# A hybrid decoder layer on one core: two orders changed, token sums taken from ScalarE's copies, and pair 2 of the first feed-forward part computed as a block step

## The chip, the core and the metric

The kernel runs on one NeuronCore of a Trainium2 chip, in float32. The metric is the device time of one execution in microseconds. The core's engines work side by side, each through its own instructions in order: TensorE (PE) multiplies and transposes, VectorE (DVE) and ScalarE (ACT) do elementwise work, GpSimd (POOL) small things, and SyncE's queue (SP) issues nearly all transfers. They wait for each other through semaphores.

## The reference

A decoder layer for 512 tokens of width 1024: a SwiGLU feed-forward part, a token mixer, and a second feed-forward part, each between RMS norms.

```python
def rms_norm(x, g):
    xf = x.astype(jnp.float32)
    y = xf * lax.rsqrt(jnp.mean(xf * xf, axis=-1, keepdims=True) + RMS_EPS)
    return (y * g.astype(jnp.float32)).astype(x.dtype)

def swiglu(x, w_gate, w_up, w_down):
    return (jax.nn.silu(x @ w_gate) * (x @ w_up)) @ w_down
...
    def compress(t, pe, w1, w2):
        tb = t[:, blk_idx] + pe[None, None, :, None, :]
```

The feed-forward width is 2816, 22 tiles of 128. The mixer projects the normed tokens once and runs two kinds of attention on the result; of it only `compress` matters here: before its matmuls it adds a small position table `pe` to the keys and values.

## The kernel before, in words

**Three products for one.** Each float32 product is made of three matmuls of rounded parts (`mm3`, L128): high by high (L130), then the tokens' low part by the weights' high part (L131), then the tokens' high part by the weights' low part (L132). So every weight block is split first (`split`, L106): ACT casts the high part (L107), DVE subtracts it to get the low part (L108). Weight blocks come by DMA into three `raw` buffers of 1 MB; their parts go to three `whi`/`wlo` pairs.

**Tokens.** The tokens are normed and transposed in four tiles of 128 (`norm_steps`, L188): squares on ACT (L139), reciprocal root on DVE and POOL (`rstd`, L142, with L148 and L152), scaling on DVE (`scale`, L198, into `tmp`), eight transposes on PE (L203), cast on ACT (L206) into `xh`, rest on DVE (L210) into `xl`.

**The feed-forward parts** (`ffn`, L277) go through 22 f-tiles in 11 pairs. A classical pair (`classical`, L391) multiplies gate and up of two f-tiles over all 512 tokens, 24 matmuls 512 wide for each product. A block pair (`strassen`, L326) treats the pair as two by two blocks, and makes 7 products in place of 8, each of 24 matmuls 256 wide. For that it needs sums of the weights' quarters (L345, L347, L351 and others, on DVE) and four sums T1 to T4 of the tokens' quarters, made once for each part by `token_sums` (L472): join high and low part of a quarter (L494), subtract (L497), split (L108). `STRASSEN` says which pairs are block pairs: in part one from pair 3, in part two from pair 2. `STEPS` says how many steps of the token sums are put behind which f-tile. For later use the quarters of the down weights are summed as well (`down_sums`, L446, L449): for some pairs in the buffer of the raw weights, for others in free slots (`early_sums`, L451).

**The opening** (from L1400 on) interleaves by hand the loads, the norms of tiles 0 to 3 and the splits of the first weights. PE starts on the first half of the tokens (tiles 0 and 1) with gate and up of f-tile 0, then does tile 2's transposes, gate of f-tile 1, tile 3's transposes, up of f-tile 1, and the second half of the tokens after that. The transposes stand in `self.pending`.

**The mixer's start** has the same form (`nsa`, L1006): four projections over the first 256 tokens, with the transposes of tiles 2 and 3 among them, while part one's end is still being normed on DVE (L633, L640). Ahead of them stands `positions` (L748): it loads the position table, transposes it on PE (L754) and copies it on DVE (L756); `block_rows` and `blocks` (L758, L768) copy the projections and add the table (L776).

**What sets the order.** The program is written in one order, and a scheduler places each instruction on its engine by it and by the buffers: a tile under one tag takes the next free buffer of that tag, and waits for its last reader. Steps inside `issue_after` are put behind a given instruction.

Of the kernel before, what the change touches and what calls it, by code (L numbers as in the profile page):

```python
# [12 lines left out]
F32 = mybir.dt.float32  # L13
# [14 lines left out]
NF = DFF // P  # L28
# [17 lines left out]
T_TAGS = ["NN"] * 3 + ["N"] + ["PT"] * 8 + ["CB"]  # L46
STRASSEN = range(3, NF // 2), range(2, NF // 2)
AHEAD = {0: 10, 1: 9}
SUM_TAGS = {2: ["KB"] * 4, 3: ["x"] * 4, 4: ["x"] * 4, 5: ["V"] * 4, 6: ["x"] * 4, 7: ["V"] * 4,
            8: ["of"] * 2 + ["V"] * 2}  # L50
STEPS = (0, 3, 3, 3, 3), (4, 4, 4)
EARLY = 5
HOLD_TAGS = ["W"] * 2 + ["Q"] * 4 + ["KA"] * 2 + ["V"] * 2 + ["CB", "ring"]
PS_BUFS = dict(S=3, T=2, V=1, F=2)
PS_TAGS = [t for t in PS_BUFS for _ in range(PS_BUFS[t])]

OPEN = ("SS", "TT", "SS", "FF")
AFTER_FFN, AFTER_MIX = ("SS", "FF", "SS", "TT"), ("SS", "TT", "FF", "SV")


class Layer:
    def __init__(self, ctx, tc, a):
        self.tc, self.nc, self.a = tc, tc.nc, a
        self.pool = ctx.enter_context(tc.tile_pool(name="sb", bufs=1))
        self.psum = ctx.enter_context(tc.tile_pool(name="ps", bufs=1, space=PSUM))
        self.nps = 0
        self.consts()

# [118 lines left out]

    def norm_steps(self, t, pre, tags):  # L188

        nc = self.nc  # L190
        xn = self.sbt("tmp", [P, D], bufs=2)
        c = slice(t * P, (t + 1) * P)
        xh, xl = self.xht, self.xlt
        pt = {}

        def scale(h, r):
            hc = slice(h * S, (h + 1) * S)
            nc.vector.scalar_tensor_tensor(xn[:, hc], self.x[2 * t + h], r, pre[h], op0=OP.mult, op1=OP.mult)  # L198

        def transpose(h):  # L200
            pt[h] = self.bank(tags[h])
            for j in range(4):
                nc.tensor.transpose(pt[h][:, j * P:(j + 1) * P], xn[:, (4 * h + j) * P:(4 * h + j + 1) * P], self.ident)  # L203

        def cast(h):
            self.last_cast = nc.scalar.copy(xh[:, 4 * h:4 * h + 4, c], pt[h].rearrange("p (j c) -> p j c", j=4)).ins  # L206

        def rest(h):
            ks = slice(4 * h, 4 * h + 4)
            self.last_rest = nc.vector.tensor_sub(xl[:, ks, c], pt[h].rearrange("p (j c) -> p j c", j=4), xh[:, ks, c].bitcast(F32)).ins  # L210
        return scale, transpose, cast, rest

    def norm_T(self, t, pre, tags, sq=None):

        r = self.rstd(sq or self.squares(t))
        scale, transpose, cast, rest = self.norm_steps(t, pre, tags)
# [60 lines left out]
    def ffn(self, n, wg, wu, wd, post, finish, xsrc, tags, nps, aside=None):  # L277
# [113 lines left out]
        def classical(f, act):  # L391
# [11 lines left out]
            nc.vector.tensor_mul(act, act, bs[1])  # L403
            if f == 1:
                sums.extend(self.token_sums())
            if 1 <= f <= len(STEPS[n]):
                with self.tc.issue_after(self.last_rest):
                    for _ in range(STEPS[n][f - 1]):
                        sums.pop(0)()
# [62 lines left out]
    def token_sums(self):  # L472


        nc = self.nc
        H = S // 2
        places = []
        for tag in T_TAGS:
            v = self.slot(tag, F32R, (P, D if tag == "NN" else S))
            places += [v[:, o:o + S] for o in range(0, v.shape[1], S)]  # L480
        self.tsum = [([], []) for _ in range(4)]
        steps = []
        for c in range(2):
            hi, lo, whole = [[v.rearrange("p (k c) -> p k c", k=2) for v in g]
                             for g in (places[8 * c:8 * c + 4], places[8 * c + 4:8 * c + 8],
                                       [self.slot("x") for _ in range(4)])]
            f1, f2, f3, f4 = whole
# [4 lines left out]
            def join(dst, i, h, c=c):  # L492
                ks, cs = slice(4 * i + 2 * c, 4 * i + 2 * c + 2), slice(h * H, (h + 1) * H)
                nc.vector.tensor_add(dst, self.xht[:, ks, cs].bitcast(F32), self.xlt[:, ks, cs].bitcast(F32))  # L494

# [510 lines left out]
    def nsa(self, fillers):  # L1006
# [306 lines left out]
    def mixer(self, post, finish):  # L1313
# [90 lines left out]
    def run(self, out):  # L1404
# [30 lines left out]
        with self.tc.manual_schedule(engines={ET.Activation, ET.DVE, ET.PE}):  # L1435
# [73 lines left out]
        self.mixer(*boundary(a["mix_post"][0], a["ffn2_pre"][0], self.x2dram, AFTER_MIX))  # L1509
        self.ffn(1, a["ffn2_w_gate"][0], a["ffn2_w_up"][0], a["ffn2_w_down"][0],  # L1510
# [31 lines left out]
```

## Time and profile before

| | |
|---|---|
| median of 3 runs | 1135.27 us (1135.04 to 1135.85) |
| the profiled execution | 1135.29 us, its span 1133.5 us, granted clock 0.999 |
| PE busy | 1118.2 us, 99% of the span |
| DVE busy | 906.9 us, 80% |
| ACT busy | 638.2 us, 56% |
| POOL busy | 75.9 us, 7% |
| chain that ended last | PE 88%, DVE 5%, ACT 2% |
| loads and stores | 206 MB, mean 182 GB/s |

A row of the timeline has the start in us from the beginning of the span, the time until the instruction's end, the engine, the line, the operation, the tile written and those read, how many alike, and in brackets the idle time ahead of it with what ended that. A matmul's end is modelled, and matmuls overlap; the distance from one start to the next is what it costs. On DVE the same holds: starts lie closer than the shown length. Busy times are averages; what a change is worth is read from the stage that it touches.

### The profile page before, as it was taken

The page shows a single profiled execution, that of the slowest core. Times are in us where ns is not written, and L with a number is a line of the kernel's source. Part 1 is how long each engine was busy: PE and PEld are TensorE (multiplying, and loading weights), DVE is VectorE, ACT ScalarE, POOL GpSimd, SP SyncE. Part 2 cuts the span into 40 slices and gives each one's busy share as a digit, 9 for nine tenths or more (in the row PEclk, how much of TensorE's full clock was granted, in tenths as well). Part 3 has the DMA queues.
Part 4 walks back from the last instruction along what each step waited for, and adds up shares of the span by engine and source line. Part 5 has one row for each costly group of instructions (what it writes and reads, how often), then busy time and mean ns, then how long its engine had stood idle before and what let it go on. Part 6 is the DMA issues. An engine that isn't in the chain of part 4 may idle for free.

```text
span 1133.5 us, 18456 instructions
## 1 busy us (share of the span) xinstructions
PE 1118.2 (99%) x6921; PEld 1000.2 (88%) x6921; DVE 906.9 (80%) x1563; ACT 638.2 (56%) x1145; POOL 75.9 (7%) x112
## 2 busy tenths in 40 slices
PE   8999999999999999999999999999999999999997
PEld 7889999998888987778888898788989999998886
DVE  6989999878666889687665687976778888979774
ACT  5435555567563788677565635645445555557562
POOL 1000000000011033343000000000000000000000
PEclk9999999999999999999999999999999999999999
DMA  9996665488763642211476758783133424357862
GB/s 319 327 300 202 186 205 179 152 274 278 278 202 92 181 126 85 58 38 55 144 247 224 253 177 291 210 296 112 67 121 122 131 87 129 122 169 240 286 225 83
DMA packets 152908, 206.01 MB, mean 182 GB/s; under 512 B 19794, under 2 KB 97906, under 8 KB 152564
## 3 DMA queue, kind: packets, MB, share of 16 engines
q1 hardware_dynamic: 152816, 204.85, 55.7%
q8 instruction: 54, 0.88, 0.3%
q14 instruction: 34, 0.28, 0.1%
q10 hardware_dynamic: 4, 0.00, 0.0%
HBM read 165.45 MB, written 39.37 MB: 181 GB/s over the span
## 4 chain that ended last, share of the span: by engine, by line
PE 88%; DVE 5%; ACT 2%; issue 2%; DMA 1%; POOL 1%; SPq 0%; POOLq 0%; DVEq 0%; ACTq 0%
PE pb_F L132 11%; PE pb_F L130 11%; PE pb_F L131 11%; PE pb_S L131 8%; PE pb_S L130 8%; PE pb_S L132 8%; PE pb_T L130 6%; PE pb_T L132 6%; PE pb_T L131 6%; PE pb_V L131 3%; PE pb_V L130 3%; PE pb_V L132 3%; PE pb_V L995 2%; PE pb_T L980 1%; DVE SP_s L730 1%
## 5 line engine op out<-in xcount | busy, mean ns | idle before, releaser
L107 ACT CAST whi<-raw 128x1024 fp32r<-128x1024 f32 (+1 forms) x215 | 219.9, 1023 | 252.5 <-issue 68.2
L108 DVE TENSOR_TENSOR wlo<-raw,whi 128x1024 fp32r<-128x1024 f32 (+1 forms) x215 | 255.0, 1188 | 98.1 <-ACT whi L107 94.5
L130 PE MATMUL pb_F<-xh_t,whi 128*128 128x512 f32 (+1 forms) x392 | 142.7, 364 | 0.9 <-DVE Q_s L1205 0.5
L132 PE MATMUL pb_F<-xh_t,wlo 128*128 128x512 f32 (+1 forms) x392 | 141.6, 361 | 0.5 <-DVE wlo L108 0.5
L131 PE MATMUL pb_F<-xl_t,whi 128*128 128x512 f32 (+1 forms) x392 | 141.8, 362 | 0.0
L107 ACT CAST whi<-tmp_t 128x1024 fp32r<-128x1024 f32 x51 | 53.5, 1048 | 59.9 <-PE pb_S L131 22.0
L130 PEld LDWEIGHTS pb_F<-xh_t,whi 128*128 128x128 f32 x392 | 74.1, 189 | 10.8 <-DVE Q_s L1205 0.7
L132 PEld LDWEIGHTS pb_F<-xh_t,wlo 128*128 128x128 f32 x392 | 74.1, 189 | 10.8 <-DVE wlo L108 1.0
L131 PEld LDWEIGHTS pb_F<-xl_t,whi 128*128 128x128 f32 x392 | 74.2, 189 | 9.6
L108 DVE TENSOR_TENSOR wlo<-tmp_t,whi 128x1024 fp32r<-128x1024 f32 x51 | 62.4, 1223 | 25.2 <-ACT whi L107 23.9
L130 PE MATMUL pb_S<-xh_t,whi 128*128 128x256 f32 (+1 forms) x240 | 73.2, 305 | 0.0
L132 PE MATMUL pb_S<-xh_t,wlo 128*128 128x256 f32 (+1 forms) x240 | 73.0, 304 | 0.0
L131 PE MATMUL pb_S<-xl_t,whi 128*128 128x256 f32 (+1 forms) x240 | 73.0, 304 | 0.0
L131 PE MATMUL pb_T<-xl_t,whi 128*128 128x256 f32 (+1 forms) x184 | 53.9, 293 | 0.0
L130 PE MATMUL pb_T<-xh_t,whi 128*128 128x256 f32 (+1 forms) x184 | 53.8, 293 | 0.0
L132 PE MATMUL pb_T<-xh_t,wlo 128*128 128x256 f32 (+1 forms) x184 | 53.8, 292 | 0.0
L971 POOL TENSOR_SCALAR SP_s<-SP_s,st_t 128x384 f32<-128x384 f32 (+2 forms) x48 | 45.8, 970 | 107.1 <-DVE st_t L907 77.3
L152 POOL TENSOR_TENSOR rs_t<-rs_t,mhalf_t 128x1 f32<-128x1 f32 x24 | 16.5, 686 | 545.2 <-DVE rs_t L148 545.2
L130 PEld LDWEIGHTS pb_S<-xh_t,whi 128*128 128x128 f32 x240 | 45.9, 191 | 1.9
L131 PEld LDWEIGHTS pb_S<-xl_t,whi 128*128 128x128 f32 x240 | 45.9, 191 | 1.9
L132 PEld LDWEIGHTS pb_S<-xh_t,wlo 128*128 128x128 f32 x240 | 45.9, 191 | 1.9
L108 DVE TENSOR_TENSOR PT_s<-pb_T,PT_s 128x512 fp32r<-128x512 f32 (+1 forms) x72 | 39.2, 559 | 6.3 <-ACT PT_s L107 5.6
(822 smaller groups left out, 3361.6 us busy)
## 6 DMA issues: line engine op xcount, KB each, us to landing
raw<-in_ffn_w_up_dram SPq DMA_DIRECT2D x36, 512.0 KB, 5.2
raw<-in_w_in_dram SPq DMA_DIRECT2D x18, 1024.0 KB, 5.6
raw<-in_ffn_w_gate_dram SPq DMA_DIRECT2D x35, 512.0 KB, 4.9
raw<-in_ffn_w_down_dram SPq DMA_DIRECT2D x14, 1024.0 KB, 5.7
raw<-tdram SPq DMA_DIRECT2D x14, 1024.0 KB, 5.2
NN_s<-in_ffn_w_down_dram SPq DMA_DIRECT2D x22, 512.0 KB, 5.1
tdram<-NN_s SPq DMA_DIRECT2D x22, 512.0 KB, 4.0
raw<-in_ffn_w_down_dram SPq DMA_DIRECT2D x6, 768.0 KB, 5.8
```

The lines of the kernel that those rows point to most:

```text
L107: self.last_cast = self.nc.scalar.copy(dsthi, src).ins
L108: self.last_rest = self.nc.vector.tensor_sub(dstlo, src, dsthi.bitcast(F32)).ins
L130: mm(out, lhi, rhi, start=start, stop=False, skip_group_check=skip)
L131: mm(out, lhi, rlo, start=False, stop=False, skip_group_check=skip)
L132: mm(out, llo, rhi, start=False, stop=stop, skip_group_check=skip)
L152: nc.gpsimd.tensor_tensor(out=r, in0=v, in1=self.mhalf, op=OP.pow)
L730: nc.vector.tensor_tensor_reduce(p, s, w, -1.0, FLOOR, OP.add, OP.min, st_m)
L971: nc.gpsimd.tensor_scalar(pp, pp, st[:, 1, t:t + 1], None, op0=OP.mult)
L980: nc.tensor.transpose(b[:, o + (t - kk) * P:o + (t - kk + 1) * P], pt[pn][:, po + kk * P:po + (kk + 1) * P], self.ident)
L995: self.nc.tensor.matmul(out[:, kk * P:S], v, pp, start=first and kk == 0 and pi == 0, stop=False, skip_group_check=True)
```

## The change

Five things are changed.

- `norm_steps` gets a fifth step, `full`: ScalarE copies the transposed tokens from PSUM into "whole" tiles (`self.whole`), two copies for each half of a token tile. In the opening it is on for tiles 2 and 3, at the mixer's end for all four.
- `token_sums` takes its quarters from there. In part one the other two quarters (tiles 0 and 1) are still joined on DVE, in slots of tag V; in part two no join is left. Its 12 steps stand behind f-tiles 1 to 3 in both parts; in part one they stood behind f-tiles 2 to 5.
- `STRASSEN` starts at pair 2 in part one too.
- In the opening the scaling of tile 2 (`norm_T(2, ...)`) is written ahead of the split of gate's second tile, and tile 3's reciprocal root ahead of the split of up's second tile.
- `positions()` is called behind the early projections, and not at the mixer's start.

```diff
-STRASSEN = range(3, NF // 2), range(2, NF // 2)
+STRASSEN = range(2, NF // 2), range(2, NF // 2)
-STEPS = (0, 3, 3, 3, 3), (4, 4, 4)
+STEPS = (0, 4, 4, 4), (0, 4, 4, 4)
+WHOLE = "VV", "xx"
...
+    def new_whole(self, half):
+        self.whole[half] = [[self.slot(tag).rearrange("p (k c) -> p k c", k=2) for _ in range(2)] for tag in WHOLE[half]]
...
+        def full(h):
+            if not whole:
+                return
+            if t % 2 == 0 and h == 0:
+                self.new_whole(t // 2)
+            for j in range(2):
+                o = self.whole[t // 2][h][j][:, :, (t % 2) * P:(t % 2 + 1) * P]
+                self.last_cast = nc.scalar.copy(o, pt[h][:, 2 * j * P:2 * (j + 1) * P].rearrange("p (j c) -> p j c", j=2)).ins
...
+            for h in range(2):
+                full(h)
         return transposes
...
-            if f == 1:
+            if f == 0:
                 sums.extend(self.token_sums())
-            if 1 <= f <= len(STEPS[n]):
+            if f < len(STEPS[n]):
                 with self.tc.issue_after(self.last_rest):
-                    for _ in range(STEPS[n][f - 1]):
+                    for _ in range(STEPS[n][f]):
                         sums.pop(0)()
...
+            def join(dst, i, c=c):
+                if joined:
+                    ks = slice(4 * i + 2 * c, 4 * i + 2 * c + 2)
+                    nc.vector.tensor_add(dst, self.xht[:, ks, 0:S // 2].bitcast(F32), self.xlt[:, ks, 0:S // 2].bitcast(F32))
...
             def s1(f1=f1, f3=f3, join=join):
-                join(f3, 0, 1)
-                join(f1, 0, 0)
+                join(f1, 0)
                 sub(f1, f3, f1)
...
         for n, (b, w) in enumerate(early):
             self.proj_T(None, b, (2 * P, S), w)
+        self.positions()
         rows = [self.block_rows(b) for b, _ in early[:2]]
...
-        self.positions()
         units, pairs = iter(range(16)), iter(range(NF // 2))
...
             sq2 = self.squares(2)
+            t2 = self.norm_T(2, g, OPEN[2], sq2, True)
             self.pre_split.append(self.ktiles(self.wsplit(self.pre_raw["g"][:, :, P:2 * P], [KT, P])))
-            t2 = self.norm_T(2, g, OPEN[2], sq2)
             sq3 = self.squares(3)
+            r3 = self.rstd(sq3)
             self.pre_split.append(self.wslots(self.pre_raw["u"][:, :, P:2 * P], "SP"))
-            t3 = self.norm_T(3, g, OPEN[3], sq3)
+            t3 = self.norm_T(3, g, OPEN[3], r=r3, whole=True)
```

How this moves the instructions is shown at three places, all on DVE. Line numbers behind the change are higher than before (L108 is L111, L198 is L204, L345 is L362).

The first place is the opening, where the scaling of token tile 2 (writes `tmp_t`) stands among the splits of the first weights (`wlo`, `SP_s`). Before:

```order
L210 TENSOR_TENSOR xl_t<-pb_T,xh_t 128x4x128
L108 TENSOR_TENSOR wlo<-raw,whi 128x1024 x2
L148 TENSOR_SCALAR rs_t<-ss_t 128x1
L198 SCALAR_TENSOR_TENSOR tmp_t<-x_s,rs_t,pb_F 128x512 x2
L108 TENSOR_TENSOR SP_s<-raw,SP_s 128x512 x2
```

And now:

```order
L216 TENSOR_TENSOR xl_t<-pb_T,xh_t 128x4x128
L111 TENSOR_TENSOR wlo<-raw,whi 128x1024
L151 TENSOR_SCALAR rs_t<-ss_t 128x1
L204 SCALAR_TENSOR_TENSOR tmp_t<-x_s,rs_t,pb_F 128x512 x2
L111 TENSOR_TENSOR wlo<-raw,whi 128x1024
L151 TENSOR_SCALAR rs_t<-ss_t 128x1
L111 TENSOR_TENSOR SP_s<-raw,SP_s 128x512 x2
```

The second split, of gate's second tile, has moved from ahead of the scaling to behind it, and tile 3's reciprocal root from behind the `SP_s` splits to ahead of them.

The second place is the first block pair, where the first weight block is split and the sums of the weights' quarters follow (`tmp_t<-raw` is a21 + a22; `PT_s`, `CB_s` are the last parts of the token sums, `W_s<-W_s,pb` the product of silu and up of the f-tile before). Before, at pair 3:

```order
L108 TENSOR_TENSOR PT_s<-x_s,PT_s 128x512
L345 TENSOR_TENSOR tmp_t<-raw 128x1024
L403 TENSOR_TENSOR ring_s<-ring_s,pb_T 128x512
L108 TENSOR_TENSOR CB_s<-x_s,PT_s 128x512
L431 TENSOR_TENSOR SP_s<-ring_s 128x256
L108 TENSOR_TENSOR wlo<-raw,whi 128x1024
L347 TENSOR_TENSOR raw<-raw 128x1024
L351 TENSOR_TENSOR tmp_t<-tmp_t,raw 128x1024
L108 TENSOR_TENSOR wlo<-raw,whi 128x1024
L403 TENSOR_TENSOR W_s<-W_s,pb_V 128x512
```

And now, at pair 2:

```order
L448 TENSOR_TENSOR SP_s<-ring_s 128x256
L111 TENSOR_TENSOR PT_s<-x_s,PT_s 128x512
L111 TENSOR_TENSOR wlo<-raw,whi 128x1024
L111 TENSOR_TENSOR CB_s<-V_s,PT_s 128x512
L466 TENSOR_TENSOR KB_s<-KB_s 128x512 x4
L362 TENSOR_TENSOR tmp_t<-raw 128x1024
L364 TENSOR_TENSOR raw<-raw 128x1024
L368 TENSOR_TENSOR tmp_t<-tmp_t,raw 128x1024
L420 TENSOR_TENSOR W_s<-W_s,pb_S 128x512
L111 TENSOR_TENSOR wlo<-raw,whi 128x1024
L447 TENSOR_TENSOR SP_s<-ring_s,W_s 128x256
```

Four sums of down weights (`KB_s`) now stand ahead of the sum a21 + a22, and the product `W_s`, which waits for PE's last f-tile, ahead of the second block's split.

The third place is the end of part one and the mixer's start (`pb_T<-pb_T,CP_s` and `x_s<-pb_T,rs_t,x_s` close part one for the third token tile, `SP_s` are the low parts of the mixer's early weights). Before:

```order
L108 TENSOR_TENSOR wlo<-raw,whi 128x1024
L633 TENSOR_TENSOR pb_T<-pb_T,CP_s 128x512
L210 TENSOR_TENSOR xl_t<-pb_S,xh_t 128x4x128 x2
L210 TENSOR_TENSOR xl_t<-pb_F,xh_t 128x4x128 x2
L148 TENSOR_SCALAR rs_t<-ss_t 128x1
L108 TENSOR_TENSOR SP_s<-raw,SP_s 128x512
L640 SCALAR_TENSOR_TENSOR x_s<-pb_T,rs_t,x_s 128x512
L640 SCALAR_TENSOR_TENSOR x_s<-of_s,rs_t,x_s 128x512
L756 COPY pe_t<-pb_T 128x32
L108 TENSOR_TENSOR SP_s<-raw,SP_s 128x512
L633 TENSOR_TENSOR pb_T<-pb_T,CP_s 128x512
```

And now:

```order
L111 TENSOR_TENSOR wlo<-raw,whi 128x1024
L111 TENSOR_TENSOR SP_s<-raw,SP_s 128x512
L652 TENSOR_TENSOR pb_T<-pb_T,CP_s 128x512
L216 TENSOR_TENSOR xl_t<-pb_S,xh_t 128x4x128 x2
L216 TENSOR_TENSOR xl_t<-pb_F,xh_t 128x4x128 x2
L151 TENSOR_SCALAR rs_t<-ss_t 128x1
L111 TENSOR_TENSOR SP_s<-raw,SP_s 128x512
L659 SCALAR_TENSOR_TENSOR x_s<-pb_T,rs_t,x_s 128x512
L659 SCALAR_TENSOR_TENSOR x_s<-of_s,rs_t,x_s 128x512
L1070 TENSOR_SCALAR W_s<-dm_t 128x512 x2
L652 TENSOR_TENSOR pb_T<-pb_T,CP_s 128x512
```

One low part of the early weights has moved ahead of the first of these `pb_T` products, the table's copy is gone from here (it comes after the projections), and two scalings of the distance table (`W_s<-dm_t`) stand in its place.

More of the change, by code (lines that the diff above doesn't have):

```diff
@@ L66, in __init__ @@
         self.nps = 0
+        self.whole = {}
         self.consts()
@@ L186, in squares, with norm_steps @@
         return [self.meansq(x, S) for x in self.x[2 * t:2 * t + 2]]
-    def norm_steps(self, t, pre, tags):
+    def new_whole(self, half):
+        self.whole[half] = [[self.slot(tag).rearrange("p (k c) -> p k c", k=2) for _ in range(2)] for tag in WHOLE[half]]
+    def norm_steps(self, t, pre, tags, whole=False):
         nc = self.nc
@@ L210, in rest, with norm_T @@
             self.last_rest = nc.vector.tensor_sub(xl[:, ks, c], pt[h].rearrange("p (j c) -> p j c", j=4), xh[:, ks, c].bitcast(F32)).ins
[L211 to L216, printed above, removed]
+        def full(h):
[6 more added lines that the diff above has]
+                self.last_cast = nc.scalar.copy(o, pt[h][:, 2 * j * P:2 * (j + 1) * P].rearrange("p (j c) -> p j c", j=2)).ins
+        return scale, transpose, cast, rest, full
+    def norm_T(self, t, pre, tags, sq=None, whole=False, r=None):
+        r = r or self.rstd(sq or self.squares(t))
+        scale, transpose, cast, rest, full = self.norm_steps(t, pre, tags, whole)
         for h in range(2):
@@ L475, in token_sums @@
         nc = self.nc
-        H = S // 2
         places = []
@@ L480, in token_sums @@
             places += [v[:, o:o + S] for o in range(0, v.shape[1], S)]
+        joined = 0 not in self.whole
+        if joined:
+            self.new_whole(0)
         self.tsum = [([], []) for _ in range(4)]
@@ L483, in token_sums @@
         for c in range(2):
[L484 to L487, printed above, removed]
+            hi, lo = [[v.rearrange("p (k c) -> p k c", k=2) for v in g]
+                      for g in (places[8 * c:8 * c + 4], places[8 * c + 4:8 * c + 8])]
+            def join(dst, i, c=c):
+                if joined:
+                    ks = slice(4 * i + 2 * c, 4 * i + 2 * c + 2)
+                    nc.vector.tensor_add(dst, self.xht[:, ks, 0:S // 2].bitcast(F32), self.xlt[:, ks, 0:S // 2].bitcast(F32))
+            whole = f1, f2, f3, f4 = [self.whole[h][i][c] for i, h in ((0, 0), (1, 1), (0, 1), (1, 0))]
             for i in range(4):
@@ L490, in token_sums @@
                     o.extend(v[:, k] for k in range(2))
-            def join(dst, i, h, c=c):
-                ks, cs = slice(4 * i + 2 * c, 4 * i + 2 * c + 2), slice(h * H, (h + 1) * H)
-                nc.vector.tensor_add(dst, self.xht[:, ks, cs].bitcast(F32), self.xlt[:, ks, cs].bitcast(F32))
             def sub(dst, x, y):
@@ L502, in s1, with s2 @@
             def s1(f1=f1, f3=f3, join=join):
-                join(f3, 0, 1)
-                join(f1, 0, 0)
+                join(f1, 0)
                 sub(f1, f3, f1)
-            def s2(f1=f1, f2=f2, f3=f3, join=join):
-                join(f2, 1, 1)
+            def s2(f1=f1, f2=f2, f3=f3):
                 sub(f3, f2, f3)
@@ L512, in s3 @@
             def s3(f2=f2, f4=f4, join=join):
-                join(f4, 1, 0)
+                join(f4, 1)
                 sub(f4, f4, f2)
+            if c:
+                self.whole = {}
             steps += [s1, s2, lambda p=parts: p(0), s3, lambda p=parts: (p(1), p(2)), lambda p=parts: p(3)]
@@ L1449, in run @@
             r0 = self.rstd(sq0)
-            scale0, transpose0, cast0, rest0 = self.norm_steps(0, g, OPEN[0])
-            scale1, transpose1, cast1, rest1 = self.norm_steps(1, g, OPEN[1])
+            scale0, transpose0, cast0, rest0, _ = self.norm_steps(0, g, OPEN[0])
+            scale1, transpose1, cast1, rest1, _ = self.norm_steps(1, g, OPEN[1])
             hi, lo = self.wpair([KT, P])
@@ L1485, in run, with boundary @@
             sq2 = self.squares(2)
+            t2 = self.norm_T(2, g, OPEN[2], sq2, True)
             self.pre_split.append(self.ktiles(self.wsplit(self.pre_raw["g"][:, :, P:2 * P], [KT, P])))
-            t2 = self.norm_T(2, g, OPEN[2], sq2)
             sq3 = self.squares(3)
+            r3 = self.rstd(sq3)
             self.pre_split.append(self.wslots(self.pre_raw["u"][:, :, P:2 * P], "SP"))
-            t3 = self.norm_T(3, g, OPEN[3], sq3)
+            t3 = self.norm_T(3, g, OPEN[3], r=r3, whole=True)
         self.pending = [t2, t3]
-        def boundary(post, pre, store, tags=None):
+        def boundary(post, pre, store, tags=None, whole=False):
             def load():
@@ L1503, in finish @@
                         self.new_xT()
-                    self.pending.append(self.norm_T(t, gain, tags[t]))
+                    self.pending.append(self.norm_T(t, gain, tags[t], None, whole))
             return load, finish
@@ L1508, in run @@
                  *boundary(a["ffn1_post"][0], a["mix_pre"][0], self.xdram, AFTER_FFN), a["x"][0], "TTSV", 6, self.distances)
-        self.mixer(*boundary(a["mix_post"][0], a["ffn2_pre"][0], self.x2dram, AFTER_MIX))
+        self.mixer(*boundary(a["mix_post"][0], a["ffn2_pre"][0], self.x2dram, AFTER_MIX, True))
         self.ffn(1, a["ffn2_w_gate"][0], a["ffn2_w_up"][0], a["ffn2_w_down"][0],
```

## The prediction

> **What bounds the kernel now.** I read the stretches first, to learn which engine sets the pace where the change works: the end of the opening (20 to 40 us), the block steps of part one (100 to 120) and those of part two (860 to 880). Columns: stretch, its length, busy us (and records) of PE, weight loads, DVE, ACT, POOL, the granted clock, DMA share, GB/s.
>
> ```profile
> 20.00:40.00 20.00, 20.00 (x163) 19.66 (x162) 18.04 (x30) 7.86 (x11) 1.27 (x3) 1.00 1.03 342
> 100.00:120.00 20.00, 20.00 (x169) 20.00 (x168) 19.08 (x25) 10.78 (x16) 0.00 (x0) 1.00 0.67 220
> 860.00:880.00 20.00, 20.00 (x169) 20.00 (x168) 17.55 (x22) 10.84 (x16) 0.00 (x0) 1.00 0.38 119
> ```
>
> TensorE is busy all the time at full clock, so only fewer matmuls or fewer of its gaps shorten the kernel. But in part one DVE has 0.92 us of slack in 20 us: a delay of DVE there soon reaches PE. In part two it has 2.45, and ACT has 9 or more in all three. The gaps that the change aims at stand in the list of PE's waits (total, times, longest):
>
> ```profile
> PE pb_S L203 <- DVE tmp_t L198: 1.3, 3, 0.7
> PE pb_T L754 <- DVE x_s L640: 1.2, 1, 1.2
> ```
>
> The sum is made against the profiled execution, 1135.29 us (span 1133.5 and 1.8 outside it), which lies 0.02 from the median 1135.27. About 0.2%, 2.3 us, is what a measurement of this kernel can tell from no change.
>
> **Pair 2 of part one as block step.** A classical pair is 4 products of 24 matmuls, 512 wide; a block pair is 7 products of 24, 256 wide. PE's timeline has the price of each: 16 starts in a row of the wide kind, then 13 of the narrow kind, where pair 3 begins.
>
> ```profile
> 61.73 0.39 PE L132 MATMUL pb_S<-xh_t,wlo 128*128 128x512 f32 x1
> ...
> 65.13 0.39 PE L132 MATMUL pb_S<-xh_t,wlo 128*128 128x512 f32 x1
> 81.67 0.28 PE L130 MATMUL pb_S<-xh_t,whi 128*128 128x256 f32 x1
> ...
> 83.11 0.28 PE L130 MATMUL pb_S<-xh_t,whi 128*128 128x256 f32 x1
> ```
>
> (65.13 − 61.73)/15 = 0.2267 us and (83.11 − 81.67)/12 = 0.120 us. So 96 × 0.2267 = 21.76 becomes 168 × 0.120 = 20.16: **−1.6 us** on the path. [...]
>
> **The opening.** Before, the scaling of the third tile (L198, its first half at 18.05) stands on DVE behind two weight splits:
>
> ```profile
> 16.03 1.23 DVE L108 TENSOR_TENSOR wlo<-raw,whi 128x1024 fp32r<-128x1024 f32 x1 [1.25 <-ACT whi L107]
> 17.18 0.21 DVE L148 TENSOR_SCALAR rs_t<-ss_t 128x1 f32<-128x1 f32 x1
> 18.05 1.41 DVE L198 SCALAR_TENSOR_TENSOR tmp_t<-x_s,rs_t,pb_F 128x512 f32<-128x512 f32 x2 [0.66 <-POOL rs_t L152]
> ```
>
> PE, done with its matmuls, waits for that:
>
> ```profile
> 17.88 0.28 PE L132 MATMUL pb_T<-xh_t,wlo 128*128 128x256 f32 x1
> 18.85 1.31 PE L203 MATMUL pb_S<-ident_t,tmp_t 128*128 128x128 f32 x8 [0.69 <-DVE tmp_t L198]
> ```
>
> Its squares are ready before that, on ACT:
>
> ```profile
> 14.54 0.19 ACT L139 ACTIVATION_READ_ACCUMULATOR junk_t<-x_s 128x1 f32 x1
> ```
>
> Now the reciprocal root can start at 14.8, DVE having been idle there for 1.25 us; with 0.87 from it to the scaling (17.18 to 18.05) the scaling runs from 15.7 to 17.0. PE then transposes at 17.88 + 0.12 = 18.0 instead of 18.85, and the second half no longer arrives late inside the eight transposes (18.85 to the next matmul is 1.07): 0.85 to 1.05, I take **−0.95**. The split of g's second tile, moved behind it, ends at 17.05 + 1.14 = 18.2 and is wanted at about 19.2, after the transposes: covered by 1.0; without that cover up to 1.2 is given back.
>
> **What the block step in pair 2 asks of DVE.** A block step needs its first weight block's split, then a21 + a22 (L345), a difference (L347), another (L351) and the second product's split, before PE gets to that product's third matmul. Before, for pair 3, that was in time:
>
> ```profile
> 74.17 1.23 DVE L345 TENSOR_TENSOR tmp_t<-raw 128x1024 f32<-128x1024 f32 x1 [2.17 <-DMA raw<-in_ffn_w_up_dram]
> ...
> 77.98 1.22 DVE L347 TENSOR_TENSOR raw<-raw 128x1024 f32<-128x1024 f32 x1
> 79.12 1.22 DVE L351 TENSOR_TENSOR tmp_t<-tmp_t,raw 128x1024 f32<-128x1024 f32 x1
> 80.40 1.23 DVE L108 TENSOR_TENSOR wlo<-raw,whi 128x1024 fp32r<-128x1024 f32 x1
> ```
>
> That split ended at 81.6 and was wanted at 81.67 + 2.88 + 0.24 = 84.8: 3.2 us to spare. Now everything before it on DVE (the token sums, two sets of weight sums, the splits of f-tiles 2 and 3) must fit in 21.76 us less. A 1024-wide operation takes 1.14 (77.98 to 79.12), a 512-wide 0.60 (345.85 to 346.45, quoted below), a 256-wide about half, 0.34. The anchor is the product of f-tile 0:
>
> ```profile
> 32.64 0.69 DVE L403 TENSOR_TENSOR ring_s<-ring_s,pb_T 128x512 f32<-128x512 f32 x1 [0.77 <-PE pb_T L132]
> ```
>
> It waits for PE, so it comes 0.95 to 1.05 earlier, at 31.6. From there DVE has 16 operations of 0.60, four of 0.34, two casts (0.9 together) and two of 1.14 until the split of f-tile 3's gate: 14.1 us, and with the split 46.9. Only then is the raw buffer free into which the block's first quarter is loaded. How long a 512 KB load takes has two rows: one alone on the queue, and the one for which L345 waited at 74.17, issued behind writes:
>
> ```profile
> raw<-in_ffn_w_up_dram SPq DMA_DIRECT2D x1, 512.0 KB, 4.0
> ```
>
> ```profile
> 67.94 0.38 SPq L336 DMA_DIRECT2D raw<-in_ffn_w_up_dram  x1
> ```
>
> 4.0 and 6.2 us. The first quarter is alone, since SP has been stopped behind it waiting for the buffer: nearest is 4.0, so it lands at 51, and after ACT's cast and two casts queued there DVE has idled about 0.9. Then: up to the sum a21 + a22 there are five operations of 0.60, one of 0.34, one of 0.60, one split of 1.14, one of 0.60 and four of 0.60, 8.1 from 48.6 with 0.9 idle, so 57.6. Behind it 3 × 1.14, the product of 0.60 and the split of 1.14 (and 0.1 for a dependence): it ends at 62.8. PE begins pair 2 at 81.67 − 21.76 − 1.0 = 58.9 and wants it at 62.0. That makes a stall of 0.8, and a little for the semaphores: **+1.0**, with 0 and 3.1 (a landing of 6.2) as ends. Later products have 1.4 or more to spare by the same count, and DVE's load in block steps stays below PE's.
>
> **Token sums from ScalarE's copies.** Four joins less on DVE in part one are in the count above; eight less in part two are 4.8 us on an engine that has 2.45 in 20 to spare, so nothing. ScalarE gets 8 and 16 copies; the nearest is a 128x256 cast from PSUM, and its gaps at the start of part two are like this one:
>
> ```profile
> 387.00 0.38 ACT L895 CAST V_s<-pb_T 128x256 fp32r<-128x256 f32 x1
> ```
>
> ```profile
> 805.82 0.62 ACT L107 CAST NN_s<-x_s 128x512 fp32r<-128x512 f32 x1 [3.49 <-DVE x_s L497]
> ```
>
> 16 × 0.38 = 6.1 us beside 3.49 and other gaps before it: **0**, at most ±0.3 if a weight cast is held up by one pair of copies.
>
> **Position table's transpose.** At the mixer's start PE waits twice:
>
> ```profile
> 349.27 0.39 PE L132 MATMUL pb_T<-CB_s,PT_s 128*128 128x512 f32 x1
> 350.89 0.24 PE L754 MATMUL pb_T<-ident_t,SP_s 32*128 32x32 f32 x1 [1.24 <-DVE x_s L640]
> ...
> 356.81 0.28 PE L132 MATMUL pb_F<-xh_t,wlo 128*128 128x256 f32 x1
> 357.17 1.10 PE L203 MATMUL pb_S<-ident_t,tmp_t 128*128 128x128 f32 x6
> ```
>
> Without the transpose the 48 matmuls start at 349.5 and end at 355.3. But what follows, the third tile's transposes, waits for a chain on DVE:
>
> ```profile
> 345.85 0.69 DVE L633 TENSOR_TENSOR pb_T<-pb_T,CP_s 128x512 f32<-128x512 f32 x1
> 346.45 1.28 DVE L210 TENSOR_TENSOR xl_t<-pb_S,xh_t 128x512 fp32r<-128x512 f32 x2
> ...
> 352.12 0.69 DVE L633 TENSOR_TENSOR pb_T<-pb_T,CP_s 128x512 f32<-128x512 f32 x1
> ...
> 356.36 1.42 DVE L198 SCALAR_TENSOR_TENSOR tmp_t<-x_s,rs_t,CP_s 128x512 f32<-128x512 f32 x2 [0.44 <-POOL rs_t L152]
> ```
>
> In the new order one more split of 0.60 stands ahead of the first L633, so all of this moves by 0.60: the scaling to 356.95, the transposes to 357.75. The wait of 1.24 isn't saved, it goes over to the transposes, and grows: **+0.6**, between −1.2 (the chain keeps up) and +0.9.
>
> The table's copy now comes behind the projections, so the sums over it (L776) start later on DVE, and the weight splits behind them get to the q projection later. PE waited there already:
>
> ```profile
> PE pb_F L132 <- DVE wlo L108: 0.5, 1, 0.5
> PE pb_F L130 <- ACT whi L107: 0.4, 1, 0.4
> ```
>
> I put **+0.4** there, as an estimate from these 0.9 us: none if the slack of DVE in this stretch takes it, as much again if not.
>
> Sum: −1.6 − 0.95 + 1.0 + 0.6 + 0.4 = −0.55, so 1135.3 − 0.6 = **1134.7 us**, with 1133.2 to 1136.2 as this case's own range.
>
> **The rivals.** *The stall is hidden* (faster): my count of DVE is contiguous over 31 us, and an error of 1 us in it removes the stall; then −1.6 − 0.95 = −2.55 and, if the mixer's chain keeps up too, −3.8: 1131.5 to 1132.8. For it speaks that four joins have left DVE; against it that the first block's load starts only when f-tile 3's gate has been split. *The block's quarters land late* (slower): the fourth quarter needed by a21 + a22 has 2.6 MB of loads and writes issued since 46.9 in front of and with it; at the 342 GB/s of the stretch from 20 to 40 that is 7.7, and with the 2.5 that a lone load takes over its own transfer (4.0 less 0.52 MB at 342, 1.5) it lands at 57.1, just ahead of the 57.6 where DVE wants it. From there each us later is a us of PE. With 6.2 for the first load (2.2 later) and another 1.2 for the queue behind it, the stall is 4.4 and the time 1138.1; it is slower than before by 0.2% from a landing of about 60.5. *The move brings nothing*: DVE is the bound around pair 2 (18.04 of 20 before, with more to do now), the 1.6 are eaten at every product and the mixer gives +1: 1135.3 to 1136.8.
>
> **How the numbers follow.** Forecast 0.36, stall hidden 0.32, late landing 0.19, nothing 0.13. Faster by over 0.2% (under 1133.0): the second and 0.03 of the forecast's tail, 0.35. Slower (over 1137.5): the third and 0.01, 0.20. Within: 0.45. The range leaves out about 0.06 below and 0.1 above: 1131.5 to 1138.1.
>
> **What would show it.** Right: the eight transposes of the third tile at 18.0; pair 2's first narrow matmul at about 58.9; one wait of PE for wlo near 62 of about 1 us; the L203 transposes of the mixer's third tile waiting 2 us or more near 357, with no wait for the table. Wrong: no wait near 62 (the count of DVE was too long), L345's counterpart waiting for a DMA past 58 (the load is the cause), or transposes at 355.3.

## The result, and the profile after

The changed kernel takes 1143.46 us (median of 5 runs, 1139.33 to 1144.28), the kernel before 1135.60 (5 runs, 1135.04 to 1136.41). The ratio is 1.0058, with an interval of 1.0043 to 1.0073: slower, where 1134.7 was forecast with a range to 1138.1. The profiled execution has a span of 1142.0 us against 1133.5, so 8.5 more, at a granted clock of 0.997 against 0.999. Here and below, the numbers leave out one slow execution, of the kernel with the order put back by force (1547.13 us at a granted clock of 0.655).

Where these 8.5 us arise is found by laying PE's timelines over each other: the start of the same instruction in both.

| PE starts | before | after | behind by |
|---|---|---|---|
| pair 2 | 59.91 | 60.50 | 0.59 |
| pair 3 | 81.67 | 82.42 | 0.75 |
| transposes of the mixer's third tile | 357.17 | 358.11 | 0.94 |
| q projection | 389.44 | 391.08 | 1.64 |
| matmul of the compression, ahead of the first heads' transposes (L814, now L833) | 407.31 | 410.09 | 2.78 |
| third of 24 matmuls among the first heads (L132, now L135) | 408.51 | 414.90 | 6.39 |
| matmuls against the compressed keys, later in the heads (L916, now L935) | 498.93 | 506.35 | 7.42 |
| end of the span | 1133.5 | 1142.0 | 8.5 |

Most of it, 5.8 us, arises among the heads, between the q projection and 500 us, of which the prediction says nothing. The list of PE's waits in the changed kernel has its main part in its first row:

```profile
PE pb_T L999 <- POOL SP_s L990: 2.8, 2, 2.1
PE pb_S L209 <- DVE tmp_t L204: 2.6, 3, 2.0
...
PE pb_V L135 <- DVE wlo L111: 1.2, 1, 1.2
PE pb_T L1266 <- DVE PT_s L111: 1.1, 1, 1.1
PE pb_V L833 <- ACT x_s L110: 0.8, 1, 0.8
```

The rows with `tmp_t` and `wlo` are the waits that were forecast: at the mixer's third tile, and for the second product of the block step in pair 2. The first is new. So is the last: 1.1 us of the 5.8 arise before PE gets to the wait for GpSimd, while it waits for the cast of a weight block (L833). The row with L1266 belongs to the last 0.9 us, which come near 700 us. On PE's timeline of the changed kernel, at that place:

```profile
411.21 0.40 PE L134 MATMUL pb_F<-xl_t,whi 128*128 128x512 f32 x1
413.73 0.33 PE L999 MATMUL pb_T<-ident_t,SP_s 128*128 128x128 f32 x1 [2.12 <-POOL SP_s L990]
414.71 0.51 PE L999 MATMUL pb_T<-ident_t,SP_s 128*128 128x128 f32 x2 [0.65 <-POOL SP_s L990]
414.90 0.75 PE L135 MATMUL pb_F<-xh_t,wlo 128*128 128x512 f32 x1
415.44 0.63 PE L133 MATMUL pb_F<-xh_t,whi 128*128 128x512 f32 x1
415.87 0.63 PE L134 MATMUL pb_F<-xl_t,whi 128*128 128x512 f32 x1
```

And in the kernel before:

```profile
413.07 0.39 PE L131 MATMUL pb_F<-xl_t,whi 128*128 128x512 f32 x1
413.29 0.39 PE L132 MATMUL pb_F<-xh_t,wlo 128*128 128x512 f32 x1
413.52 1.03 PE L980 MATMUL pb_T<-ident_t,SP_s 128*128 128x128 f32 x8
```

Two things are to be seen. The order differs: before, all eight transposes of the first head's probabilities (L980, now L999) stand behind the 24 matmuls of a gate projection (`pb_F`), and GpSimd's scaling of these probabilities has time to finish. Now three of them stand behind the second of these matmuls, and 22 matmuls that could run wait with them. And the matmuls behind the wait start 0.43 us apart (415.44 to 415.87), where those of the kernel before start 0.22 apart (413.07 to 413.29). The windows of the changed kernel show the clock there (PEclk, the column after five pairs of busy times):

```profile
60.00:80.00 20.00, 18.75 (x151) 18.22 (x151) 19.84 (x23) 10.64 (x14) 0.00 (x0) 1.00 0.93 292
100.00:120.00 20.00, 20.00 (x169) 20.00 (x169) 19.38 (x26) 10.76 (x16) 0.00 (x0) 1.00 0.70 220
412.00:414.00 2.00, 0.27 (x1) 0.14 (x1) 2.00 (x6) 1.10 (x3) 2.00 (x3) 1.00 1.05 356
414.00:416.00 2.00, 1.35 (x6) 1.10 (x6) 2.00 (x4) 2.00 (x5) 1.98 (x2) 0.73 0.37 119
416.00:418.00 2.00, 2.00 (x6) 1.52 (x5) 0.85 (x2) 0.51 (x1) 2.00 (x2) 0.50 0.22 41
418.00:420.00 2.00, 2.00 (x9) 1.64 (x8) 0.00 (x0) 0.00 (x0) 1.36 (x2) 0.91 1.04 221
```

PE is idle most of 412 to 414, then TensorE is granted half its clock until a little after 418. The first row answers to the prediction's doubt about pair 2: PE loses 1.25 us from 60 to 80, with DVE busy for 19.84 of 20.

### The profile page after: what moved, and what is told of

Same layout as the page of the kernel before. It is cut to its first block, busy times and chain, and to the rows that moved or that the text cites. A ratio compares the mean times of both kernels' runs of the same rounds, so it can differ in the third digit from the quotient of the medians.

```text
span 1142.0 us, 18642 instructions
## 1 busy us (share of the span) xinstructions
PE 1120.3 (98%) x6993; PEld 1005.2 (88%) x6993; DVE 909.6 (80%) x1561; ACT 649.4 (57%) x1177; POOL 78.5 (7%) x112
## 4 chain that ended last, share of the span: by engine, by line
PE 83%; DVE 7%; ACT 3%; DMA 3%; issue 2%; POOL 1%; SPq 0%; DVEq 0%; POOLq 0%; ACTq 0%
PE pb_F L133 10%; PE pb_F L135 10%; PE pb_F L134 10%; PE pb_S L133 7%; PE pb_S L134 7%; PE pb_S L135 7%; PE pb_T L133 6%; PE pb_T L134 6%; PE pb_T L135 6%; PE pb_V L135 2%; PE pb_V L133 2%; PE pb_V L134 2%; PE pb_V L1014 2%; PE pb_T L999 1%; PE pb_S L743 1%
## 5 line engine op out<-in xcount | busy, mean ns | idle before, releaser
L111 DVE TENSOR_TENSOR wlo<-raw,whi 128x1024 fp32r<-128x1024 f32 (+1 forms) x215 | 255.4, 1189 | 95.0 <-ACT whi L110 92.6
L135 PE MATMUL pb_F<-xh_t,wlo 128*128 128x512 f32 (+1 forms) x392 | 142.4, 363 | 0.5 <-DVE wlo L111 0.5
L110 ACT CAST whi<-tmp_t 128x1024 fp32r<-128x1024 f32 x54 | 56.6, 1049 | 61.4 <-PE pb_S L134 26.0
L111 DVE TENSOR_TENSOR wlo<-tmp_t,whi 128x1024 fp32r<-128x1024 f32 x54 | 66.1, 1223 | 24.1 <-ACT whi L110 22.8
L135 PEld LDWEIGHTS pb_F<-xh_t,wlo 128*128 128x128 f32 x392 | 74.5, 190 | 11.1 <-DVE wlo L111 1.0
L135 PE MATMUL pb_S<-xh_t,wlo 128*128 128x256 f32 (+1 forms) x240 | 72.2, 301 | 0.0
L990 POOL TENSOR_SCALAR SP_s<-SP_s,st_t 128x384 f32<-128x384 f32 (+2 forms) x48 | 48.4, 1022 | 111.0 <-ACT whi L110 51.2
L133 PE MATMUL pb_T<-xh_t,whi 128*128 128x256 f32 x184 | 52.9, 287 | 0.0
L134 PE MATMUL pb_T<-xl_t,whi 128*128 128x256 f32 x184 | 52.7, 286 | 0.0
L135 PE MATMUL pb_T<-xh_t,wlo 128*128 128x256 f32 x184 | 52.6, 286 | 0.0
L749 DVE CUSTOM_DVE_ANT_0 SP_s<-pb_S,W_s 128x128 f32<-128x128 f32 (+2 forms) x92 | 37.8, 442 | 12.6 <-PE pb_S L744 10.4
L135 PEld LDWEIGHTS pb_S<-xh_t,wlo 128*128 128x128 f32 x240 | 45.9, 191 | 1.6
```

Of the source, the lines that this page charges most:

```text
L110: self.last_cast = self.nc.scalar.copy(dsthi, src).ins
L111: self.last_rest = self.nc.vector.tensor_sub(dstlo, src, dsthi.bitcast(F32)).ins
L133: mm(out, lhi, rhi, start=start, stop=False, skip_group_check=skip)
L134: mm(out, lhi, rlo, start=False, stop=False, skip_group_check=skip)
L135: mm(out, llo, rhi, start=False, stop=stop, skip_group_check=skip)
L749: nc.vector.tensor_tensor_reduce(p, s, w, -1.0, FLOOR, OP.add, OP.min, st_m)
```

## The experiments

Each kernel was timed in five rounds beside the kernel before, except the last, which is one execution. Theory A: the table's move changes PE's order among the heads, and that is the loss. Theory B, the prediction's own: the move costs about 1 us at the mixer's start and the q projection, and the rest lies elsewhere.

**The move alone.** The kernel before, with:

```diff
             self.proj_T(None, b, (2 * P, S), w)
+        self.positions()
         rows = [self.block_rows(b) for b, _ in early[:2]]
...
-        self.positions()
         units, pairs = iter(range(16)), iter(range(NF // 2))
```

> Kernel before with the position table's transpose moved behind the early projections, and nothing else changed. Theory A (the move changes PE's order among the attention heads: three transposes that need GpSimd's scaled probabilities come ahead of 22 matmuls): 3.5 to 7 us slower than before, so 1139 to 1142.5, with PE waiting 2 us or more at those transposes and half-speed matmuls behind the wait. Theory B (the move costs only what the prediction put there, the mixer's start and the q projection): about 1.0 us slower, 1136.6, and no such wait.

1142.38 us against 1135.98, ratio 1.0053 (1.0037 to 1.0069): as slow as the whole change. Its profile has the same order and the same wait, but this execution kept the clock (1.00 in every window from 402 to 420):

```profile
409.42 0.40 PE L131 MATMUL pb_F<-xl_t,whi 128*128 128x512 f32 x1
411.95 0.33 PE L980 MATMUL pb_T<-ident_t,SP_s 128*128 128x128 f32 x1 [2.14 <-POOL SP_s L971]
412.93 0.44 PE L980 MATMUL pb_T<-ident_t,SP_s 128*128 128x128 f32 x2 [0.65 <-POOL SP_s L971]
413.12 0.48 PE L132 MATMUL pb_F<-xh_t,wlo 128*128 128x512 f32 x1
413.44 0.40 PE L130 MATMUL pb_F<-xh_t,whi 128*128 128x512 f32 x1
```

This one took 1139.22 us. The six executions of this kernel differ, and the time goes with the mean granted clock:

```
us     1139.22  1140.07  1142.18  1142.57  1144.29  1144.53
clock    0.999    0.999    0.997    0.996    0.995    0.995
```

So the move costs 3.2 to 3.9 us in the profiled execution (against the median before, and against the profile before), and up to 5.3 more in the others. The clock can account for these, by an estimate from the table and the profile's span: a mean lower by 0.004 over 1137 us is 9 us at half the clock, in which 4.5 us of work are lost. Where the slower executions of this kernel lose it isn't shown, since the profile is of the fastest. In the profile the move costs 0.9 us up to the q projection, where the prediction had put 1.0, 0.4 from there to the wait, and 3.1 at the wait. Theory A holds; B's 1136.6 doesn't.

**The whole change without the move.** The changed kernel, with the two edits above undone.

> Changed kernel with the position table's transpose put back to the mixer's start. Theory A: the 8 us come from that move, so what is left is the opening (-0.95) and pair 2 (about 0): 1134 to 1135.5, no wait for GpSimd among the heads. Theory B: most of the loss lies elsewhere, in pair 2 and the clock: 1141 to 1143.

1136.67 us against 1135.98, ratio 1.0009 (0.9999 to 1.0019). The wait among the heads is gone. But the time lies 1.2 above the top of what A expected. Its profile shows where: at 500 us PE is still 0.2 ahead of the kernel before, so opening and pair 2 together bring next to nothing, and then a wait of 2.6 near 710 (0.4 in the kernel before) puts it behind:

```profile
PE pb_S L1300 <- DVE PT_s L111: 3.1, 2, 2.6
707.07 1.05 ACT L110 CAST whi<-raw 128x1024 fp32r<-128x1024 f32 x1 [3.93 <-DMA raw<-in_w_nsa_o_dram]
```

The second row, from ScalarE's timeline, says why: a weight block landed late there, far from all that the change touches. Whether it does so in the other executions isn't shown.

**The opening alone.** The kernel before, with the opening's edits of the change's diff only.

> Kernel before with only the opening's two orders changed. If the opening's step was priced rightly: 1134.6 (-0.95), the third tile's transposes at 18.0 us. If the new order itself brings the slow first matmuls seen in the changed kernel's profile (spacing 0.215 where before has 0.120, 1.2 us): 1135.5 to 1136.5.

1134.60 us, ratio 0.9989 (0.9980 to 0.9997). The opening is worth what was forecast, within its interval. In its profile the eight transposes start at 17.55 with no wait, and the first matmuls are 0.12 us apart; in the changed kernel's profile they are 0.21 apart, so that isn't the order's doing.

**The order put back by force.** The changed kernel, with the transposes held behind the last matmul of that projection (`unit_mm`, noted in `merge_unit`):

```diff
+                    with self.tc.issue_after(self.unit_mm):
-                    nc.tensor.transpose(b[:, o + (t - kk) * P:o + (t - kk + 1) * P],
-                                        pt[pn][:, po + kk * P:po + (kk + 1) * P], self.ident)
+                        nc.tensor.transpose(b[:, o + (t - kk) * P:o + (t - kk + 1) * P],
+                                            pt[pn][:, po + kk * P:po + (kk + 1) * P], self.ident)
```

> Changed kernel with the first unit's transposes of probabilities held behind the 22 matmuls, as they stood before. Theory A: the wait of 2 us at these transposes and the half clock behind it go, 1136.5 to 1138.5; the late start of the chain of the heads (about 1 us by then) stays. Theory B: no change, 1142 to 1144.

1138.41 us, ratio 1.0027 (1.0016 to 1.0038), where the change has 1.0058: about 3.5 us of its 6.6 are gone. The table is moved here as in the change; only the order of PE differs. What PE does from 405 to 425 us, in the kernel before, in the change, and in this one:

```profile
405.00:425.00 20.00, 19.62 (x117) 16.60 (x117) 15.74 (x45) 15.46 (x38) 8.76 (x9) 1.00 0.58 146
```

```profile
405.00:425.00 20.00, 15.88 (x76) 12.11 (x75) 12.95 (x39) 13.93 (x32) 8.64 (x6) 0.91 0.46 118
```

```profile
405.00:425.00 20.00, 19.31 (x105) 15.41 (x104) 16.01 (x45) 15.75 (x37) 10.73 (x9) 1.00 0.60 146
```

Of PE's lost 4.1 us 0.7 are left, and the clock of 0.91 is back at 1.00. From the q projection to 500 us PE now loses 1.0 us, where the change lost 5.8. The move's other cost is still there: from 340 to 500 us PE falls behind by 1.9 (0.87 to 2.79), at the mixer's start, at the q projection and in that last 1.0.

This kernel also showed the block step in a harsher light. The opening went well (its third tile's transposes start 0.92 us ahead of before), and yet pair 3 begins 0.86 late: pair 2 took 23.8 us in place of 21.76. Its DVE rows ahead of pair 2:

```profile
54.87 0.69 DVE L111 TENSOR_TENSOR PT_s<-x_s,PT_s 128x512 fp32r<-128x512 f32 x1 [2.90 <-ACT PT_s L110]
55.48 1.22 DVE L111 TENSOR_TENSOR wlo<-raw,whi 128x1024 fp32r<-128x1024 f32 x1
56.62 0.69 DVE L111 TENSOR_TENSOR CB_s<-V_s,PT_s 128x512 fp32r<-128x512 f32 x1
```

DVE waits 2.90 us for ACT, which casts the block's first quarter first, and that had landed only at 53.2, 6.2 us after its issue. Theories C to F below are about pair 2.

**Pair 2 classical.** The kernel without the move, with `STRASSEN = range(3, ...)` for part one.

> Changed kernel with the table's transpose back at the mixer's start and pair 2 classical again; the opening's orders and ScalarE's copies stay. Theory C (the block step in pair 2 costs its own gain and more, the copies cost nothing): as the opening alone, 1134.0 to 1135.2. Rival D (the copies on ScalarE are what costs): no better than with the block step, 1136 to 1137.

1135.70 us, ratio 1.0002 (0.9994 to 1.0011). By the ratios that is 0.8 us better than with the block step (1.0009) and 1.5 worse than the opening alone (0.9989). The intervals overlap both times, and 1135.7 lies between what C and D expected: the times don't decide. In its profile pair 3 begins 0.8 ahead of the kernel before and pair 4 0.4 late, and PE waits 0.77 us in pair 3 for ScalarE's copy of a product (L370). What holds this copy up is seen on DVE and on ScalarE:

```profile
79.17 1.23 DVE L362 TENSOR_TENSOR tmp_t<-raw 128x1024 f32<-128x1024 f32 x1 [3.13 <-DMA raw<-in_ffn_w_up_dram]
86.62 0.62 ACT L110 CAST KA_s<-ring_s 128x512 fp32r<-128x512 f32 x1 [2.66 <-DVE ring_s L449]
```

ScalarE stood idle 2.66 us ahead of it, waiting for DVE, and DVE's sum a21 + a22 had waited for a load that was issued at 74.28, where the kernel before issues it at 67.94. The copies of the opening are long over by then (21 to 26 us). So D isn't what this profile shows; why the load is issued later wasn't settled.

**Two edits for pair 2.** The order on DVE ahead of the wait, in the changed kernel: four sums of pair 9's down weights, then a21 + a22, two differences, the product of f-tile 3, and the split that PE waits for.

```profile
57.10 2.87 DVE L466 TENSOR_TENSOR KB_s<-KB_s 128x512 f32<-128x512 f32 x4
59.88 1.22 DVE L362 TENSOR_TENSOR tmp_t<-raw 128x1024 f32<-128x1024 f32 x1
61.14 1.23 DVE L364 TENSOR_TENSOR raw<-raw 128x1024 f32<-128x1024 f32 x1
62.28 1.22 DVE L368 TENSOR_TENSOR tmp_t<-tmp_t,raw 128x1024 f32<-128x1024 f32 x1
63.42 0.68 DVE L420 TENSOR_TENSOR W_s<-W_s,pb_S 128x512 f32<-128x512 f32 x1
64.02 1.22 DVE L111 TENSOR_TENSOR wlo<-raw,whi 128x1024 fp32r<-128x1024 f32 x1
```

Theory E takes this chain for the cause, theory F the landing of the quarters. One edit takes the sums out, one takes a write of 1 MB out of the queue between the quarters, and a third kernel has both; all three are without the move.

```diff
-AHEAD = {0: 10, 1: 9}
+AHEAD = {0: 10}
```

> Changed kernel with the table's transpose back, and the early sums for pair 9 (four operations on DVE, 2.4 us, and their transfers) not made ahead in pair 1 but in pair 9 itself. Theory E (the wait inside pair 2 is DVE's chain in order: every operation ahead of a21 + a22 delays it): the sum starts up to 2.4 earlier until the landing of the fourth quarter holds it, 1.2 to 2.4 less wait, 1134.3 to 1135.5. Theory F (the wait is the landing of the weights alone): no change, 1136 to 1137.

1137.05 us, ratio 1.0013 (1.0004 to 1.0021): no gain in the time. In the profile the sum starts 1.25 earlier than without the edit (57.52, not 58.77), where a landing holds it, and pair 2 takes 20.83, 0.9 less than the classical pair of the kernel before:

```profile
57.52 1.23 DVE L362 TENSOR_TENSOR tmp_t<-raw 128x1024 f32<-128x1024 f32 x1 [1.54 <-DMA raw<-in_ffn_w_up_dram]
```

The gain is given back behind pair 9, in which its sums are now made: pair 10 takes 22.0 us in place of 20.16 (below).

```diff
+            if p == 1:
+                self.late = p, r
+            else:
-            nc.sync.dma_start(self.tdram[p], r.rearrange("p e (h d) -> p (e h) d", h=2))
+                nc.sync.dma_start(self.tdram[p], r.rearrange("p e (h d) -> p (e h) d", h=2))
...
                 ab.append((r[:, 0], r[:, 1]))
+            if n == 0 and p == 2:
+                q, v = self.late
+                nc.sync.dma_start(self.tdram[q], v.rearrange("p e (h d) -> p (e h) d", h=2))
```

> Changed kernel with the table's transpose back, and the write of pair 1's sums (1 MB) issued behind the block step's four loads and not between them. Theory E: the third and fourth quarters land 2.7 us earlier, but DVE gets to their sum no earlier: 1136 to 1137, within 0.5 of the kernel without this edit. Theory F: 1134 to 1135.

1136.26 us, ratio 1.0009 (1.0000 to 1.0018): within 0.5 of the kernel without this edit. The quarters land earlier (the second at 53.1 and not 56 to 57), and yet PE waits 1.9 us in pair 2, and then has half its clock:

```profile
66.00:68.00 2.00, 2.00 (x11) 2.00 (x11) 2.00 (x3) 0.22 (x1) 0.00 (x0) 0.50 1.02 286
```

Pair 2 takes 23.8 us here. F falls, as far as the landing alone goes. E wasn't right in all either: the sum starts at 56.35, 2.4 earlier than without the edit, since only one of pair 9's four sums stands ahead of it now. The other three stand behind it, and the split that PE waits for starts at 62.50, only 0.4 earlier.

> Both of these edits. Theory E: DVE's chain is 2.4 shorter and no landing holds it; the second product's split is done at about 60.6 and wanted at 61.9, the wait is gone and pair 2 gains its 1.6: 1132.5 to 1133.8, faster than the opening alone. Theory F: as with the write moved alone, 1134 to 1135.

1134.67 us, ratio 0.9994 (0.9985 to 1.0003). In the profile pair 2 is what a block step should be: PE is busy throughout, and it takes 20.3 us.

```profile
60.00:80.00 20.00, 20.00 (x167) 19.87 (x166) 18.14 (x22) 10.36 (x14) 0.00 (x0) 1.00 0.83 264
```

So both hold pair 2, DVE's chain first and the landing right behind it; E holds for the place. Its time was missed by 0.9, since a new wait stands at 225 us, in pair 10, behind pair 9's sums. DVE itself waits for a load ahead of that:

```profile
PE pb_V L135 <- DVE wlo L111: 1.4, 1, 1.4
215.93 1.23 DVE L368 TENSOR_TENSOR tmp_t<-raw 128x1024 f32<-128x1024 f32 x1 [1.64 <-DMA raw<-in_ffn_w_up_dram]
```

**Pair 9's sums in pair 10.** DVE had 14 of 20 us to do there before.

```diff
-            weight_sums(p)
+            if p != 9:
+                weight_sums(9 if (n, p) == (0, 10) else p)
```

> The kernel with the table's transpose back, pair 9's sums not made ahead and pair 1's write issued late, and now pair 9's sums made in pair 10, where DVE has room (14 of 20 us), and not in pair 9, where the profile showed 1.5 us given back. Theory E (each block step's waits are DVE's load in its own stretch): 1132.7 to 1133.8, 1.5 below the kernel without this edit, and faster than before and than the opening alone. Rival (the loss at pair 9 was of another kind, a transfer): 1134.5 or more.

1133.32 us against 1135.52, ratio 0.9985 (0.9976 to 0.9994): 2.2 us faster than the kernel before, and 1.35 less than without this edit, as E expected. Whether it is faster than the opening alone (0.9989) isn't clear of the noise. The edit moves the sums together with the buffer of raw weights that they use, so it doesn't tell DVE's load from the late load of the row above. From 50 to 240 us one short wait of PE is left:

```profile
PE pb_S L133 <- ACT pb_S L376: 0.4, 1, 0.4
```

**The changed kernel once more.**

> The changed kernel once more, for its profile. Theory A with the clock: the order among the heads is the same, so PE waits for GpSimd 2 us or more again at the same three transposes; what differs from execution to execution is whether the matmuls behind it run at half speed (spacing 0.43 us where 0.227 is the rule), and the time follows the mean granted clock, 4.5 us from 0.999 to 0.995. Rival: the executions differ in the length of waits, at the same clock.

1142.73 us at a clock of 0.995. The same order, but the wait for GpSimd is now 1.2 in all: PE was held up earlier, by a cast that waits for a weight block (L833, 1.5). What was expected of the length of waits is not what happened: PE's waits shift from execution to execution as well as the clock. Behind the wait for GpSimd the clock stayed at 1.00 (414 to 422). It was lost behind the mixer's start, after a wait of 2.0, and behind the 1.5 at L833 (last row):

```profile
356.00:358.00 2.00, 0.10 (x1) 0.10 (x2) 1.27 (x4) 1.12 (x4) 0.55 (x1) 1.00 0.71 262
358.00:360.00 2.00, 1.99 (x11) 1.75 (x12) 1.27 (x3) 0.92 (x2) 0.55 (x1) 0.67 0.03 8
360.00:362.00 2.00, 2.00 (x12) 2.00 (x11) 1.97 (x4) 0.25 (x1) 0.00 (x0) 0.50 0.00 0
...
410.00:412.00 2.00, 1.96 (x9) 1.81 (x9) 2.00 (x9) 2.00 (x9) 0.00 (x0) 0.50 0.33 59
```

## Why the prediction was wrong, point by point

**The heads: the step that is missing.** "Position table's transpose" follows the move to the mixer's start and to the q projection, and ends there. It took the order of PE behind that for unchanged, so what the move does there was put at nothing, without a reason. The scheduler had placed three transposes ahead of 22 matmuls, and PE, which takes its instructions in order, held all 22 for the slowest of the three (in the change the second matmul starts at 411.21, the third at 414.90). The kernel with the move alone is 6.4 us slower than before, and its profile, of an execution at full clock that is 3.9 longer than the profile before, has 3.1 at this wait. With the order put back by force, what PE loses between the q projection and 500 us falls from 5.8 to 1.0. No rival named it. It was to be read in PE's order of both kernels, and the profile of before had the other half: GpSimd's three scalings begin at 408.8 there and take 3.0 us, so anything that needs them ahead of 412 would wait.

**The clock.** The price of a wait on PE was taken as its length. In three of the twelve profiles TensorE had half its clock for 3.4 us at a time between 20 and 1120 us, four times in all, each time behind waits of 1.5 to 2.1 us: once in the change's first profile (0.73, 0.50 and 0.91 from 414 to 420, behind 2.1), twice in its second (0.67 and 0.50 from 358 to 362, behind 2.0; 0.97, 0.50 and 0.68 from 408 to 414, behind 1.5), and once in pair 2 of the kernel with the late write (0.50 from 66 to 68, behind 1.9). Each time 1.7 us of work are lost, half of the 3.4. What halves the clock isn't shown, and the length of the wait alone doesn't tell when: behind one of 2.14 (411.95 above) it stayed at 1.00.

**The opening: right.** −0.95 was forecast; alone it gave −1.4, with an interval that reaches from −0.3 to −2.3. PE's timeline has it closer: from the last matmul ahead of the third tile's transposes to the first behind them it takes 2.04 us before (17.88 to 19.92), 0.92 with the opening alone (17.43 to 18.35) and 0.91 in the change (19.59 to 20.50), so −1.1. The scaling ran at 15.88 (15.7 forecast). In the changed kernel's profile this gain is used up ahead of time, because the first matmuls were 0.21 us apart there until about 15, which put PE 1.2 further behind. That is no fault of the order, which the kernel with the opening alone has too. That it is the clock isn't shown: the windows give 1.00 for this stretch, but the trace's record of the clock begins only at 15.6, where the slow matmuls end.

**Pair 2: the mechanism right, the size off.** "That makes a stall of 0.8, and a little for the semaphores: +1.0" is the term. Measured is 1.8 in the change (60.50 to 82.42 is 21.92, less 20.16) and 3.6 in the kernel with the forced order. Of the 2.6 by which 3.6 exceeds the forecast, 2.2 are the landing: 6.2 us, the end of the range, and not the 4.0 of "alone on the queue". In the other seven profiles with the block step it was 4.2 to 4.8. The block's gain of 1.60 itself was right: pairs 3 to 10 take 20.16 us without waits. One reading was wrong: not "the fourth quarter" is needed by a21 + a22 but the third, which landed at 57.43 in the kernel without the early sums, where the sum starts at 57.52 and the fourth landed at 58.94. What the text missed is that two things can hold the same split, DVE's chain and the load behind it. With a load of about 4.2 the opening's saving goes through: without the move pair 2 begins 1.0 earlier than in the change (59.47), and pair 3 1.1 earlier. With the load of 6.2 it is waited away: pair 2 begins 1.8 earlier than in the change, and pair 3 0.1 later.

**The mixer's start: right.** A wait of 2 us or more near 357 was forecast, and net +0.6. The profile has 1.96 at 358.11, and net +0.2 (0.75 to 0.94). That the wait for the table is handed to the transposes holds. From there to the q projection the loss is 0.7 where 0.4 was put.

**The copies: nothing was forecast.** In part two nothing is lost: in the change PE is as far behind at 1120 us as at 806. In part one the kernel with pair 2 classical shows a late load, as said, and not the copies; that it is 1.5 short of the opening alone stays open.

**The slower rival** had the right sign and the wrong place: late landings in pair 2, at 4.4. One does occur, in the kernel with the forced order, and the stall there is 3.6. In the change itself the load took 4.3, and the stall was 1.8.

## What to carry to other kernels

When a scheduler sets the order, a moved instruction can change it far from where it stood: compare the order of the engine that bounds the kernel over its whole length, and price each instruction that now stands ahead of work that could run. Before adding gains in a row, ask what is late next: whether the second keeps the first can hang on one load. And count what a wait on TensorE costs behind it: in the change's first profile one of 2.1 us was followed by 3.4 us at half the clock, 1.7 us of work.

## What the runs showed of the hardware

The kernel with the move alone, where PE waits 2.14 us among the heads, took 1139.2 to 1144.5 us in six executions, in step with a mean clock of 0.999 to 0.995. The best kernel ran from 1132.0 to 1136.4 (11 executions, 0.999 to 0.996). The four stretches at half the clock were 3.4 us long, behind waits of 1.5 to 2.1 us; behind the 2.14 the clock stayed at 1.00. The same 512 KB load, of pair 2's first quarter, took 4.2 to 6.2 us from issue to landing in eight profiles (6.2 in the kernel with the forced order, 4.2 in the one without the move). In the change it was issued at 48.75, 2.8 us after the end of the issue before it on SyncE's queue (at 45.14, 0.85 long), and took 4.3.
